# An encoder on one core: the memory's tokens turned by VectorE from row tile 4 on, one row tile at a time

## The chip, the cores and the metric

The kernel runs on one core of a Trainium2 chip. A core has a matrix engine (TensorE, PE in the profile), an elementwise engine (VectorE, DVE), an engine for activations (ScalarE, ACT), a general one (GpSimd, POOL) and one that here only issues transfers (SyncE, SP). Each works through its own instructions in order; they meet through semaphores. The metric is the device time of the whole program in microseconds, lower is better.

## The reference

The program is a two-layer encoder for 256 rows of 2048 numbers. Each layer projects the normed rows, runs three groups of heads (a gated convolution, a differential attention, an attention into 256 memory rows), and adds the projected result.

```python
def rmsnorm(x, g):
    y = x * lax.rsqrt(jnp.mean(x * x, axis=-1, keepdims=True) + EPS)
    return y * g

for l in range(DEPTH):                          # DEPTH = 2
    proj = rmsnorm(x, norm_g[l]) @ w_in[l]      # 256 x 2048 by 2048 x 7168
    y_a = short_gated_conv(a_x, a_b, a_c, conv_w[l], conv_b[l]) * silu(a_g)
    y_d = rmsnorm(diff_attention(q, k, v, lam, slopes), ...) * (1.0 - lam_init) * silu(d_g)
    mkv = rmsnorm(mem, mem_norm_g[l]) @ w_mem_kv[l]     # 256 x 2048 by 2048 x 1024
    mk, mv = rmsnorm(mkv[..., :512], mem_k_norm_g[l]), mkv[..., 512:]
    y_m = memory_attention(rmsnorm(m_q, mem_q_norm_g[l]), mk, mv) * silu(m_g)
    x = x + concat(y_a, y_d, y_m) @ w_out[l]    # 2048 x 2048
```

The change concerns `mkv`, which the kernel computes for both layers before anything else, since the memory is the same for both.

## The kernel before

All products run in a split form: an operand is cut into a high part and a low part (what the high part leaves over), and three products high x high, low x high and high x low are added up. ScalarE makes the high parts, VectorE the low ones.

The memory stage is a loop over `g` = 0 to 31: 16 row tiles of 128 rows of the contraction for layer 0, then 16 for layer 1 (`NG` = 32, `k = g % 16`). For each `g` TensorE does 12 products of 512 columns: two halves of the 1024 columns (keys, values), two tiles of 128 memory rows, three product kinds. Both operands of a row tile must be ready:

- the tokens, transposed, as `memT` (high and low part), made once in layer 0 and kept for layer 1. `token_parts` calls `split_T`, which casts the high part on ScalarE (L261) and subtracts on VectorE (L262).
- the weights. `weights(g + 4)` starts the load of a row tile (512 KB) into one of four `raw` buffers; `w_parts` scales by the norm's gain and makes the high part on ScalarE (L738, tile `hi`) and the low part on VectorE (L739, tile `lo`), each into one of four buffers.

The operands of row tile `g + 2` are made while TensorE works on `g` (`operands`: first the tokens, then the weights). Up to `g` = 2 the loop is written out apart, with the operands of the next tile only.

The tokens come in two ways. Row tiles 0 to 7 (`k < DEALT`, with `DEALT` = 8) are loaded in their natural layout into `xs`, and TensorE transposes them into PSUM (`turned`, L744, two instructions for a row tile). Row tiles 8 to 15 are loaded as strips of 32 rows into a tile `xt` (`strips_of`, four transfers of 128 KB for four row tiles), and one VectorE transpose of 128x1024, which turns blocks of 32x32, yields four row tiles (`strips_turned`, L634, tile `xf`). These row tiles take every fourth row of a block of 512, and their weights and gains (`gm_dealt`) are loaded in the same arrangement. The turn is a task: it is started at `g` = 2 and `g` = 4 and runs some steps later. The rows of `xs` are also needed for the sum of squares, which ScalarE makes in four pairs (`mem_squares`, L681) at `g` = 4, 8, 11 and 13.

At the end of a layer's row tiles the order of the products differs: for `k` = 14 and 15 the first half (keys) of both comes first and the second halves of both behind, and for the first two row tiles of layer 1 likewise, so that ScalarE can empty the first layer's accumulators (`empty_keys`, L782, `empty_values`, L788) meanwhile.

From `g` = 12 on the same loop loads the strips of `x`, turns them in the same way (`x_turned`) and makes `xT` for the first layer's projections; `x_next` does it again at the end of layer 0.

Nearly all of this is pinned: each engine gets its instructions in the order in which the program writes them. SP issues the loads in program order too, and a load into a buffer that is still read holds up those behind it.

Of the kernel before, what the change touches and what calls it, by code (L numbers as in the profile page):

```python
# [37 lines left out]
NA = P // B  # L38
PAIR_EVERY = 9
QT = NB // P  # L40
DEALT = 8


C_X, C_B, C_C, C_G = 0, 768, 1536, 2304
# [5 lines left out]
def encoder(ctx: ExitStack, tc: tile.TileContext, x, mem, norm_g, w_in, conv_w, conv_b,  # L50
# [21 lines left out]
    def nm(s):  # L72
        uid[0] += 1
        return f"{s}_{uid[0]}"
# [54 lines left out]
    def g_norm(l, k):  # L129
        return gx[:, l * KT + k:l * KT + k + 1]  # L130
# [83 lines left out]
    def later(g, n):  # L214
        due[id(g)] = chunk[0] + n
        return g
# [40 lines left out]
    def split_T(dst, k, src, gain, pin=False):  # L257

        hi, lo = dst[:, 0, k, :], dst[:, 1, k, :]
        if gain is None:  # L260
            both = (nc.scalar.copy(hi, src),  # L261
                    nc.vector.tensor_tensor(lo, src, hi.bitcast(F32), ALU.subtract))  # L262
        else:
            both = (nc.scalar.activation(hi, src, AF.Copy, scale=gain),
                    nc.vector.scalar_tensor_tensor(lo, src, gain, hi.bitcast(F32), ALU.mult, ALU.subtract))
        if pin:
            for i in both:
                tc.keep_in_program_order(i)
        made.add((id(dst), k))
# [352 lines left out]
    def strips_of(src, at_once=1):  # L622

        st = tmp.tile([P, SEQ // B, B * QT], F32, tag="e", name=nm("xt"))
        for b in range(NA):
            pin(nc.sync.dma_start(
                st[b * B:(b + 1) * B], src[:, b * B * QT:(b + 1) * B * QT].rearrange("(n p) r -> p n r", p=B)))
            if (b + 1) % at_once == 0 and b + 1 < NA:
                yield
        return st  # L630

    def strips_turned(st):
        whole = tmp.tile([P, QT, SEQ], F32, tag="sh", name=nm("xf"))
        pin(nc.vector.transpose(whole.rearrange("p j (n i) -> p j n i", i=B),  # L634
                                st.rearrange("p n (c j) -> p j n c", j=QT)))
        return whole

    def x_turned(dst, l, q, src, at_once):


        st = yield from strips_of(src, at_once)
        yield 2
        whole = strips_turned(st)
        yield
        for j in range(QT):
            split_T(dst, q * QT + j, whole[:, j], g_norm(l, q * QT + j), pin=True)
            if j % 2:
                yield

    def x_next(dst, l, q):  # L650

# [92 lines left out]
            pin(nc.tensor.transpose(pt[:, t * P:(t + 1) * P], xs[:, t, k * P:(k + 1) * P], ident))  # L744
        return pt

    dealt = {}

    def mem_turned(q, at_once):
        st = yield from strips_of(mem[:, q * NB:(q + 1) * NB], at_once)  # L750
        yield 2
        dealt[q] = strips_turned(st)

    def token_parts(g):
        if g < KT:
# [2 lines left out]
    def operands(g):  # L758
        token_parts(g)
        w_parts(g)  # L760
# [32 lines left out]
    def x_natural(c, t):  # L793
        pin(nc.sync.dma_start(xs[:, t, c * NB:(c + 1) * NB], x[t * P:(t + 1) * P, c * NB:(c + 1) * NB]))

    TOKENS = {0: 4, 1: 6, 8: 8, 9: 10, 10: 12, 11: 14}
    MEM_STRIPS = {2: 2, 4: 3}
    X_STRIPS = {12: 0, 16: 1, 20: 2, 24: 3}
    X_NATURAL = {14: (0, 0), 17: (0, 1), 20: (1, 0), 22: (1, 1), 24: (2, 0), 26: (2, 1), 28: (3, 0), 29: (3, 1)}
    X_SQUARES = {19: 0, 25: 1, 29: 2}  # L800
# [1 line left out]
    def beside(g):  # L802


        if g + 4 < NG:
            if g in TOKENS:
                tokens(TOKENS[g], 2)
            weights(g + 4)
        if g in MEM_STRIPS:
            tasks.append(later(mem_turned(MEM_STRIPS[g], 2 if g == 2 else 1), 1))  # L810
        if g >= 2:
            for dst, src in islice(constants, 1):
                pin(nc.sync.dma_start(dst, src))
        if g in X_STRIPS:
            q = X_STRIPS[g]
            tasks.append(later(x_turned(xT, 0, q, x[:, q * NB:(q + 1) * NB], 1), 1))
        if g in (4, 8, 11, 13):
            mem_squares((4, 8, 11, 13).index(g))
        if g == 6:
            distance(1)  # L820
        if g == 13:
            tasks.append(later(mem_stats(), 1))
        if g == 21:
            tasks.append(later(rest_of_constants(), 1))
        if g in X_NATURAL:
            x_natural(*X_NATURAL[g])
        if g in X_SQUARES:
            for t in range(NT):
                x_square(X_SQUARES[g], t)
# [22 lines left out]
    weights(2, NB, NB)  # L852
    tokens(3, 1)
    weights(3)
    warm(6)
    distance(0)
    pv = ps_t.tile([P, NB], F32, tag="t", name="pva")
# [13 lines left out]
    for g in range(3):  # L871
        if g > 0:
            products(g, 0, FIRST + REST)
        w_parts(g + 1, 0, NB)
        products(g, 1, FIRST)
        token_parts(g + 1)
        w_parts(g + 1, NB, NB)
        beside(g)
        products(g, 1, REST)
        run_side()  # L880
    for g in range(3, NG):
        l, k = divmod(g, KT)
        ends = k >= KT - 2
        begins = l > 0 and k < 2
        products(g, 0, FIRST)
        if begins and k == 1:
            empty_values(0)
        for n in (4, 5) if g == 3 else (g + 2,):
            if n < NG:
                operands(n)  # L890
        products(g, 0, REST)
        beside(g)
        if k == KT - 1:
            empty_keys(l)
        if not (ends or begins):
            products(g, 1, FIRST + REST)
        elif k in (1, KT - 1):
            for n in (g - 1, g):
                products(n, 1, FIRST + REST)
        run_side()  # L900
# [199 lines left out]
```

## Time and profile before

| | us |
|---|---|
| median of 3 runs | 920.24 (919.87 to 920.91) |
| profiled execution | 920.2 |
| its span, first to last instruction | 918.3 |
| TensorE busy | 912.9 (99%) |
| VectorE busy | 675.0 (74%) |
| ScalarE busy | 501.3 (55%) |
| granted TensorE clock | 1.00 throughout |

In the profile's rows a name like `memT<-xf` is the written tile and those read; `L262` is a line of the kernel before. The memory stage takes about the first 95 us of the span, of which layer 0's sixteen row tiles take the first 51. The busy shares are means over the whole program; in a single stage another engine can be the one that is waited for.

### The profile page before, as it was taken

The numbers are of one execution on the slowest core, as the hardware profiler recorded it, in microseconds if no ns is written. First come the engines' busy times: TensorE is split into PE (matmuls) and PEld (weight loads), VectorE is DVE, ScalarE is ACT, GpSimd is POOL, SyncE is SP. The second block draws the span as 40 slices with busy tenths as digits, with TensorE's granted clock in tenths as the row PEclk, the third lists the DMA queues.
The fourth block names the chain that finished last, engine by engine and source line by source line (L and its number), as shares of the span: only waits on it lengthen the run. The fifth ranks groups of instructions, "written<-read, shape, count | busy, mean of one in ns | idle before, by whom it ended". The sixth has DMA issues, their size and how long they took to land.

```text
span 918.3 us, 12315 instructions
## 1 busy us (share of the span) xinstructions
PE 912.9 (99%) x4176; PEld 758.8 (83%) x4176; DVE 675.0 (74%) x1197; ACT 501.3 (55%) x770; POOL 7.0 (1%) x18
## 2 busy tenths in 40 slices
PE   9999999999999999999999999999999999999998
PEld 6888888888888888888888888888888888888886
DVE  5889978867898777458676757878898677458652
ACT  6766745675545654446455544568555554446431
POOL 0001000000000000000000000000000000000000
PEclk9999999999999999999999999999999999999999
DMA  8999878876769997989677767886888897978662
GB/s 283 290 292 299 273 247 233 252 212 184 186 216 256 239 263 227 240 267 260 221 259 246 235 199 219 234 233 185 236 230 222 242 249 215 281 231 252 211 221 74
DMA packets 254242, 216.11 MB, mean 235 GB/s; under 512 B 131982, under 2 KB 181476, under 8 KB 254180
## 3 DMA queue, kind: packets, MB, share of 16 engines
q1 hardware_dynamic: 252020, 211.78, 80.2%
q0 software_dynamic: 672, 2.10, 0.6%
q10 hardware_dynamic: 1488, 1.46, 0.5%
q8 instruction: 32, 0.52, 0.2%
q14 instruction: 30, 0.25, 0.1%
HBM read 194.32 MB, written 20.97 MB: 234 GB/s over the span
## 4 chain that ended last, share of the span: by engine, by line
PE 99%; DMA 0%; ACT 0%; ACTq 0%; DVE 0%; DVEq 0%; issue 0%
PE acc L311 28%; PE acc L312 28%; PE acc L310 28%; PE acc L773 10%; PE po L443 2%; PE s L551 1%; PE s L550 1%; PE s L603 1%; DMA raw<-in_w_mem_kv_dram 0%; PE pt L744 0%; ACT hi L738 0%; ACTq L842 0%; DVE xs L1061 0%; DVEq L1095 0%; PE pvb L150 0%
## 5 line engine op out<-in xcount | busy, mean ns | idle before, releaser
L290 DVE TENSOR_TENSOR lo<-raw,hi 128x1024 fp32r<-128x1024 f32 x288 | 351.6, 1222 | 181.2 <-ACT hi L289 176.4
L289 ACT CAST hi<-raw 128x1024 fp32r<-128x1024 f32 x288 | 302.4, 1052 | 327.1 <-PE acc L312 263.7
L311 PE MATMUL acc<-lo,xT 128*128 128x512 f32 x896 | 349.0, 390 | 0.0
L312 PE MATMUL acc<-hi,xT 128*128 128x512 f32 x896 | 348.7, 389 | 0.0
L310 PE MATMUL acc<-hi,xT 128*128 128x512 f32 x896 | 348.4, 391 | 0.0
L312 PEld LDWEIGHTS acc<-hi,xT 128*128 128x128 f32 x896 | 168.2, 188 | 34.9
L310 PEld LDWEIGHTS acc<-hi,xT 128*128 128x128 f32 x896 | 168.2, 188 | 33.9
L311 PEld LDWEIGHTS acc<-lo,xT 128*128 128x128 f32 x896 | 168.3, 188 | 33.5
L310 PE MATMUL acc<-hi,yT 128*128 128x512 f32 x256 | 99.6, 389 | 0.0
L311 PE MATMUL acc<-lo,yT 128*128 128x512 f32 x256 | 99.6, 389 | 0.0
L312 PE MATMUL acc<-hi,yT 128*128 128x512 f32 x256 | 99.6, 389 | 0.0
L773 PE MATMUL acc<-hi,memT 128*128 128x512 f32 (+1 forms) x260 | 70.5, 389 | 0.7 <-ACT hi L738 0.7
L773 PEld LDWEIGHTS acc<-hi,memT 128*128 128x128 f32 x260 | 47.9, 188 | 10.8 <-ACT hi L738 1.2
L311 PEld LDWEIGHTS acc<-lo,yT 128*128 128x128 f32 x256 | 48.0, 188 | 10.1
L310 PEld LDWEIGHTS acc<-hi,yT 128*128 128x128 f32 x256 | 48.0, 188 | 10.0
L312 PEld LDWEIGHTS acc<-hi,yT 128*128 128x128 f32 x256 | 48.0, 188 | 9.8
L773 PE MATMUL acc<-lo,memT 128*128 128x512 f32 (+1 forms) x130 | 39.7, 387 | 0.0
L773 PEld LDWEIGHTS acc<-lo,memT 128*128 128x128 f32 x130 | 24.3, 188 | 5.0
L739 DVE SCALAR_TENSOR_TENSOR lo<-raw,cva,hi 128x1024 fp32r<-128x1024 f32 (+2 forms) x21 | 21.4, 1027 | 5.9 <-ACT hi L738 4.8
L561 ACT ACTIVATE e<-e,mx 128x256 f32<-128x256 f32 x48 | 23.8, 498 | 1.4 <-DVE mx L557 1.3
L739 DVE SCALAR_TENSOR_TENSOR lo<-raw,gm_dealt,hi 128x1024 fp32r<-128x1024 f32 x16 | 20.5, 1279 | 4.1 <-ACT hi L738 3.4
L738 ACT ACTIVATE hi<-raw,cva 128x1024 fp32r<-128x1024 f32 (+2 forms) x21 | 19.6, 947 | 5.1 <-DMA raw<-in_w_mem_kv_dram 5.1
(155 smaller groups left out, 634.5 us busy)
## 6 DMA issues: line engine op xcount, KB each, us to landing
raw<-in_w_in_dram SPq DMA_DIRECT2D x192, 512.0 KB, 4.3
raw<-in_w_out_dram SPq DMA_DIRECT2D x64, 512.0 KB, 4.5
raw<-in_w_in_dram SPq DMA_DIRECT2D x64, 256.0 KB, 4.4
raw<-in_w_mem_kv_dram SPq DMA_DIRECT2D x29, 512.0 KB, 5.9
d<-sh SPq DMA_DIRECT2D x80, 128.0 KB, 3.9
sh<-d SPq DMA_DIRECT2D x64, 128.0 KB, 3.8
d<-yn SPq DMA_DIRECT2D x40, 64.0 KB, 3.9
yn<-d SPq DMA_DIRECT2D x40, 64.0 KB, 3.3
```

Source lines behind the costliest of these rows:

```text
L289: nc.scalar.copy(hi, raw)
L290: nc.vector.tensor_tensor(lo_, raw, hi.bitcast(F32), ALU.subtract)
L310: nc.tensor.matmul(acc[t], sh, hi, start=first, stop=False)
L311: nc.tensor.matmul(acc[t], sh, lo, start=False, stop=False)
L312: nc.tensor.matmul(acc[t], sl, hi, start=False, stop=last)
L443: nc.tensor.matmul(po[:, t, :], eT[:, i, t, k, :], v[:, k, h * P:(h + 1) * P], start=k == 0, stop=k == NT - 1)
L550: nc.tensor.matmul(s[c][:, i, :], qi, k_first(yT, c, h), start=True, stop=False)
L551: nc.tensor.matmul(s[c][:, i, :], qi, k_second(yT, k2, c, h), start=False, stop=True)
L561: nc.scalar.activation(e[:, c, i], e[:, c, i], AF.Exp, bias=mx[:, c, i:i + 1], accum_out=sm[:, c, i:i + 1])
L738: pin(nc.scalar.activation(hi, raw, AF.Copy, scale=gain))
L739: pin(nc.vector.scalar_tensor_tensor(lo, raw, gain, hi.bitcast(F32), ALU.mult, ALU.subtract))
L773: pin(nc.tensor.matmul(accs[l, half][t][:, at:at + n], memT[:, token_part, k, t * P:(t + 1) * P], p, start=k == 0 and at == 0 and token_pa ...
```

## The change

`DEALT` becomes 4: row tiles 4 to 7 also come in strips, and TensorE transposes only row tiles 0 to 3. Their strips are loaded ahead of the loop, right behind the weights of row tile 3, and one of the two gain loads with them. VectorE no longer turns four row tiles of the memory at once: `mem_turn(k)` turns a single one (128x256), row tile 4 at `g` = 2 and each later one behind the operands of the row tile before it. The strips of `x` are turned in halves of two row tiles (128x512). The natural tokens of row tiles 4 to 7, now needed for the squares alone, are loaded later, and the squares move to `g` = 4, 10, 12 and 14.

```diff
-DEALT = 8
+DEALT = 4
...
-    def strips_turned(st):
-        whole = tmp.tile([P, QT, SEQ], F32, tag="sh", name=nm("xf"))
-        pin(nc.vector.transpose(whole.rearrange("p j (n i) -> p j n i", i=B),
-                                st.rearrange("p n (c j) -> p j n c", j=QT)))
-        return whole
+    def turn_strips(whole, st, at, n):
+        pin(nc.vector.transpose(whole.rearrange("p j (n i) -> p j n i", i=B)[:, at:at + n],
+                                st.rearrange("p n (c j) -> p j n c", j=QT)[:, at:at + n]))
...
-        whole = strips_turned(st)
-        yield
-        for j in range(QT):
-            split_T(dst, q * QT + j, whole[:, j], g_norm(l, q * QT + j), pin=True)
-            if j % 2:
-                yield
+        whole = whole_tile()
+        for j in range(0, QT, 2):
+            turn_strips(whole, st, j, 2)
+            yield
+            for i in (j, j + 1):
+                split_T(dst, q * QT + i, whole[:, i], g_norm(l, q * QT + i), pin=True)
...
+    def mem_strips(q, at_once):
+        strips_in[q] = yield from strips_of(mem[:, q * NB:(q + 1) * NB], at_once)
+
+    def mem_turn(k):
+        q, j = divmod(k, QT)
+        if j == 0:
+            dealt[q] = whole_tile()
+        turn_strips(dealt[q], strips_in[q], j, 1)
...
-    TOKENS = {0: 4, 1: 6, 8: 8, 9: 10, 10: 12, 11: 14}
-    MEM_STRIPS = {2: 2, 4: 3}
+    TOKENS = {4: 4, 7: 6, 8: 8, 9: 10, 10: 12, 11: 14}
+    MEM_STRIPS = {2: 2, 5: 3}
...
-        if g in (4, 8, 11, 13):
-            mem_squares((4, 8, 11, 13).index(g))
+        if g in (4, 10, 12, 14):
+            mem_squares((4, 10, 12, 14).index(g))
...
     weights(3)
+    for _ in mem_strips(1, NA):
+        pass
+    for dst, src in islice(constants, 1):
+        pin(nc.sync.dma_start(dst, src))
...
         products(g, 1, FIRST)
+        if g + 2 == DEALT:
+            mem_turn(DEALT)
         token_parts(g + 1)
...
                 operands(n)
+            if n + 1 < KT:
+                mem_turn(n + 1)
```

How this moves the instructions is seen best in the built order. First VectorE, before, around the operands of row tiles 6 to 9 (`memT` from `pt` or `xf` is the tokens' low part, `lo` the weights' low part, the STREAM_TRANSPOSE the turn of the strips `xt`):

```order
L739 SCALAR_TENSOR_TENSOR lo_295<-raw_242,cva,hi_294 128x1024
L262 TENSOR_TENSOR memT_105<-pt_319,memT_105 128x256
L739 SCALAR_TENSOR_TENSOR lo_325<-raw_276,cva,hi_324 128x1024
L634 STREAM_TRANSPOSE xf_341<-xt_249 128x1024
L262 TENSOR_TENSOR memT_105<-xf_341,memT_105 128x256
L739 SCALAR_TENSOR_TENSOR lo_349<-raw_302,gm_dealt,hi_348 128x1024
L262 TENSOR_TENSOR memT_105<-xf_341,memT_105 128x256
L739 SCALAR_TENSOR_TENSOR lo_372<-raw_332,gm_dealt,hi_371 128x1024
```

In the changed kernel VectorE has this around the operands of row tiles 3 to 6:

```order
L740 SCALAR_TENSOR_TENSOR lo_235<-raw_126,cva,hi_234 128x512
L636 STREAM_TRANSPOSE xf_240<-xt_128 128x256
L262 TENSOR_TENSOR memT_105<-pt_242,memT_105 128x256
L740 SCALAR_TENSOR_TENSOR lo_235<-raw_126,cva,hi_234 128x512
L262 TENSOR_TENSOR memT_105<-xf_240,memT_105 128x256
L740 SCALAR_TENSOR_TENSOR lo_264<-raw_196,gm_dealt,hi_263 128x1024
L636 STREAM_TRANSPOSE xf_240<-xt_128 128x256
L262 TENSOR_TENSOR memT_105<-xf_240,memT_105 128x256
L740 SCALAR_TENSOR_TENSOR lo_271<-raw_221,gm_dealt,hi_270 128x1024
L636 STREAM_TRANSPOSE xf_240<-xt_128 128x256
```

Before, one turn stands between the operands of row tiles 7 and 8 and none between 8 and 9; now a turn of a quarter of the size stands between those of every two row tiles from 3 on, each behind the low part of the weights and ahead of the low part of the tokens that it yields. On ScalarE, which makes the high parts, the same place (row tiles 3 to 5) reads before

```order
L738 ACTIVATE hi_229<-raw_126,cva 128x512
L261 CAST memT_105<-pt_254 128x256
L738 ACTIVATE hi_259<-raw_191,cva 128x1024
L261 CAST memT_105<-pt_263 128x256
L738 ACTIVATE hi_268<-raw_217,cva 128x1024
L261 CAST memT_105<-pt_289 128x256
```

and now

```order
L261 CAST memT_105<-pt_242 128x256
L739 ACTIVATE hi_234<-raw_126,cva 128x512
L261 CAST memT_105<-xf_240 128x256
L739 ACTIVATE hi_263<-raw_196,gm_dealt 128x1024
L261 CAST memT_105<-xf_240 128x256
L739 ACTIVATE hi_270<-raw_221,gm_dealt 128x1024
```

The order is the same: each cast of tokens stands between the high part of the weights before it and that of its own row tile. What is new is that the casts read `xf`, which VectorE turned, where they read `pt`, which TensorE transposed. The third place is SP's queue around the weights of row tiles 3 to 6 (`raw_126` are those of row tile 3), before

```order
L731 DMA raw_126<-in_w_mem_kv_dram 128x1024
L721 DMA xs<-in_mem_dram 128x2x256
L731 DMA raw_191<-in_w_mem_kv_dram 128x1024
L721 DMA xs<-in_mem_dram 128x2x256
L731 DMA raw_217<-in_w_mem_kv_dram 128x1024
L731 DMA raw_242<-in_w_mem_kv_dram 128x1024
L813 DMA gm_dealt<-in_mem_norm_g_dram 128x2x4
L626 DMA xt_249<-in_mem_dram 32x8x128 x2
```

and now

```order
L732 DMA raw_126<-in_w_mem_kv_dram 128x1024
L626 DMA xt_128<-in_mem_dram 32x8x128 x4
L863 DMA gm_dealt<-in_mem_norm_g_dram 128x3x4
L732 DMA raw_196<-in_w_mem_kv_dram 128x1024
L732 DMA raw_221<-in_w_mem_kv_dram 128x1024
L818 DMA gm_dealt<-in_mem_norm_g_dram 128x3x4
L732 DMA raw_249<-in_w_mem_kv_dram 128x1024
```

The loads of natural tokens around the weights of row tile 4 are gone from here, and four strips and a gain load stand ahead of those weights.

More of the change, by code (lines that the diff above doesn't have):

```diff
@@ L630, in strips_of, with whole_tile @@
         return st
-    def strips_turned(st):
-        whole = tmp.tile([P, QT, SEQ], F32, tag="sh", name=nm("xf"))
-        pin(nc.vector.transpose(whole.rearrange("p j (n i) -> p j n i", i=B),
-                                st.rearrange("p n (c j) -> p j n c", j=QT)))
-        return whole
+    def whole_tile():
+        return tmp.tile([P, QT, SEQ], F32, tag="sh", name=nm("xf"))
+    def turn_strips(whole, st, at, n):
+        pin(nc.vector.transpose(whole.rearrange("p j (n i) -> p j n i", i=B)[:, at:at + n],
+                                st.rearrange("p n (c j) -> p j n c", j=QT)[:, at:at + n]))
     def x_turned(dst, l, q, src, at_once):
@@ L745, in turned @@
         return pt
[L747 to L752, printed above, removed]
+    dealt, strips_in = {}, {}
+    def mem_strips(q, at_once):
[5 more added lines that the diff above has]
+        turn_strips(dealt[q], strips_in[q], j, 1)
     def token_parts(g):
@@ L809, in beside @@
         if g in MEM_STRIPS:
-            tasks.append(later(mem_turned(MEM_STRIPS[g], 2 if g == 2 else 1), 1))
-        if g >= 2:
+            tasks.append(later(mem_strips(MEM_STRIPS[g], 2), 1))
+        if g >= 1:
             for dst, src in islice(constants, 1):
@@ L816, in beside @@
             tasks.append(later(x_turned(xT, 0, q, x[:, q * NB:(q + 1) * NB], 1), 1))
-        if g in (4, 8, 11, 13):
-            mem_squares((4, 8, 11, 13).index(g))
+        if g in (4, 10, 12, 14):
+            mem_squares((4, 10, 12, 14).index(g))
         if g == 6:
             distance(1)
-        if g == 13:
+        if g == 14:
             tasks.append(later(mem_stats(), 1))
```

## The prediction

> **What bounds the kernel now.** I read the page first: the busy times and the chain that ended last.
>
> ```profile
> span 918.3 us, 12315 instructions
> PE 912.9 (99%) x4176; PEld 758.8 (83%) x4176; DVE 675.0 (74%) x1197; ACT 501.3 (55%) x770; POOL 7.0 (1%) x18
> PE 99%; DMA 0%; ACT 0%; ACTq 0%; DVE 0%; DVEq 0%; issue 0%
> ```
>
> TensorE is busy for 912.9 of 918.3 us and holds 99% of the chain. So there are only two ways to move the time: take work from TensorE, or make it wait. The second view is the chain in order of time, in the memory stage (start, us, what).
>
> ```profile
> 14.05 1.40 PE acc L773 x6
> 15.45 0.44 PE pt L744 x4
> 15.89 2.77 PE acc L773 x12
> 18.66 0.22 PE pt L744 x2
> 18.88 2.77 PE acc L773 x12
> 21.66 0.22 PE pt L744 x2
> 21.88 45.84 PE acc L773 x202
> ```
>
> From 21.88 on 202 products take 45.84 us, 0.227 each, and the 12 of a row tile 2.72 us. This is the pace that the other engines must hold. The third view is the timeline of DVE and ACT where the turn of tiles 12 to 15 stands today (start, us, and in brackets the idle time before and what ended it).
>
> ```profile
> 33.67 1.28 DVE L739 SCALAR_TENSOR_TENSOR lo<-raw,gm_dealt,hi 128x1024 fp32r<-128x1024 f32 x1 [0.63 <-ACT hi L738]
> 34.87 1.98 DVE L634 STREAM_TRANSPOSE xf<-xt 128x1024 f32<-128x1024 f32 x1
> 36.88 0.41 ACT L261 CAST memT<-xf 128x256 fp32r<-128x256 f32 x1 [3.25 <-DVE xf L634]
> 37.20 1.15 ACT L738 ACTIVATE hi<-raw,gm_dealt 128x1024 fp32r<-128x1024 f32 x1
> 38.38 1.29 DVE L739 SCALAR_TENSOR_TENSOR lo<-raw,gm_dealt,hi 128x1024 fp32r<-128x1024 f32 x1 [0.63 <-ACT hi L738]
> 38.54 1.15 ACT L738 ACTIVATE hi<-raw,gm_dealt 128x1024 fp32r<-128x1024 f32 x1
> 39.58 0.42 DVE L262 TENSOR_TENSOR memT<-xf,memT 128x256 fp32r<-128x256 f32 x1
> 39.60 0.62 ACT L681 ACTIVATE msq<-xs 128x512 f32<-128x512 f32 x1
> 40.82 0.39 ACT L261 CAST memT<-xf 128x256 fp32r<-128x256 f32 x1
> ```
>
> Here is a closed path. The weight's low part on DVE (33.67) must finish before the turn behind it (34.87); ACT's cast of the tokens waits for the turn (3.25 us idle); the weight's high part follows the cast on ACT; the next low part on DVE waits for that high part. Today the path closes once in four tiles: the low parts of tile 11 and tile 12 start 4.71 us apart, and the three other tiles of the quarter make it up.
>
> **The change part by part.**
>
> *Removed: eight transposes on TensorE* (tiles 4 to 7, two each). From 15.45 to 21.88 lie 6.43 us with 24 products; 24 x 0.227 = 5.45, so the eight cost 0.98 us with the breaks in the pipeline. They lie on the chain: -0.98.
>
> *Added: a turn of 128x256 behind every tile's low part*, twelve in place of two of 128x1024. This is the part that counts. No turn of 128x256 is in the trace; the nearest rows are these (us in all, mean ns).
>
> ```profile
> L634 DVE STREAM_TRANSPOSE xf<-xt 128x1024 f32<-128x1024 f32 x10 | 20.1, 2009 | 0.0
> L405 DVE STREAM_TRANSPOSE sh<-sh 128x1024 f32<-128x1024 f32 x10 | 12.4, 1238 | 0.0
> L534 DVE STREAM_TRANSPOSE yn<-yn 128x512 f32<-128x512 f32 x10 | 7.0, 700 | 0.0
> ```
>
> The plain turns cost 1238 for 1024 elements and 700 for 512, so 162 ns of each are fixed. A quarter of the 2009 with the fixed part kept is (2009 - 162) / 4 + 162 = 624 ns. The bounds: 502 if nothing were fixed, 431 if the small turn ran at the plain pace (162 + 1076 / 4). Nothing below that is likely, since all these rows move the same kind of data. I take 624, because the plain rows show the fixed part directly. [...]
>
> Now the path closes in every tile, since the order puts tile n+1's turn behind tile n's low part, and the cast of tile n+1 behind tile n's high part. Its period, from the third view: 1.20 from low part to turn (33.67 to 34.87); the turn; 1.53 from the turn's end (34.87 + 1.98 = 36.85) over cast and high part to the next low part (38.38). That is 2.73 + 0.62 = 3.35 us, against TensorE's 2.72. Each tile loses 0.63 us, and nothing later in the loop gives it back. The cover that hid the turn so far was the three tiles without one.
>
> How much lead there is at the start comes from the rows around tile 3.
>
> ```profile
> 12.13 1.49 DVE L739 SCALAR_TENSOR_TENSOR lo<-raw,cva,hi 128x512 fp32r<-128x512 f32 x2 [0.20 <-ACT hi L738]
> 14.36 0.73 ACT L738 ACTIVATE hi<-raw,cva 128x512 fp32r<-128x512 f32 x1
> 14.83 0.62 PE L773 MATMUL acc<-hi,memT 128*128 128x512 f32 x2
> ```
>
> The turn of tile 4 stands behind the low parts that end at 13.62. ACT is free for tile 4's cast at 15.09, makes the high part from 15.41 to 16.56, and DVE's low part of tile 4 starts at 16.59. TensorE begins tile 3 at 14.83, so without waits tile 4 at 17.55, tile 14 at 44.77, and, as the second halves of tiles 14 and 15 are put off behind both first halves, tile 15 only 6 products (1.36) later, at 46.13. It needs a tile's low part after 4 products, 0.91 later: for tile 15 at 47.04. The low part of tile 15 starts at 16.59 + 11 x 3.354 = 53.48 and ends 1.28 later, at 54.76. So TensorE comes out **7.7 us late**: 11 x 0.63 lost, 1.36 for the short tile 14, less 0.6 of lead at tile 4. After tile 15 no turn follows and the path opens.
>
> *What follows at once.* Behind tile 15 ACT has to empty the accumulators of the first layer before TensorE may fill them for the second.
>
> ```profile
> 48.48 1.07 ACT L782 COPY kraw<-acc 128x512 f32<-128x512 f32 x2
> 49.44 0.65 ACT L360 ACTIVATE sq<-kraw 128x512 f32<-128x512 f32 x1
> 51.54 1.27 ACT L788 ACTIVATE mv<-acc,stm 128x512 f32<-128x512 f32 x2
> ```
>
> With no lead left, ACT goes from the high part of tile 15 (ends near 53.4) through high parts 16 to 18, the moved pair of squares, both copies and two squares (3 x 1.06 + 1.22 + 1.07 + 2 x 0.6) (a high part 1.06 from start to start, 38.54 to 39.60) to about 60.1 and gives the first value accumulator back near 60.7, the second near 61.4. TensorE, 14 products after 54.76, wants them 12 products later, at 60.7. The second is late: **+0.5**, between 0 and 1.3 (both copies).
>
> *Moved: tokens and weights in SP's queue.* Four strip loads and one gain load now stand ahead of the weights of tile 4.
>
> ```profile
> 6.39 0.43 SPq L721 DMA_DIRECT2D xs<-in_mem_dram  x1
> 9.92 3.32 SPq L731 DMA_DIRECT2D raw<-in_w_mem_kv_dram  x2
> xt<-in_mem_dram SPq DMA_DIRECT2D x8, 128.0 KB, 5.9
> DMA to landing us min/median/max: 4.9/5.8/7.3
> ```
>
> The strips take the place of the load at 6.39; at about 0.45 each the last goes out near 8.2 and lands 5.9 later, at 14.1. The turn is over at 14.7, ahead of ACT at 15.09: no cost. At the slowest landing, 7.3, the path starts 1.0 later, and the weights of tile 4, out near 9.2, can then be as late: 0 to +1.1, I take 0. The weights of tile 5 went out at 9.92 already and keep that place. Later strips wait for a turn to free their buffer, and the weights queued behind them on SP are used 10 us later: 0.
>
> *Squares and the rest.* A pair of squares takes 1.22 on ACT (39.60 to 40.82), and ACT idles 1.9 in each turn of the closed path (low part and turn): 0; without that cover the three moved pairs would cost up to 3.7. The halves of x add a fixed 0.16 to each of eight quarters, 1.3 if all lay bare. There the waits between 465 and 535 us (who waits for whom, us, times, longest) show ACT ahead of TensorE, waiting for it to free buffers:
>
> ```profile
> ACT hi L289 <- PE acc L312: 27.8, 18, 1.7
> ```
>
> So that is 0 as well.
>
> **Sum.** 918.3 - 0.98 + 7.7 + 0.5 = 925.5 us of span. The profiled execution took 920.2, 1.9 around its span, and the median of the runs is 920.24; so 927.4 us, 0.8% slower.
>
> **The rivals.**
>
> *The turn stays hidden* (not slower). If DVE did the turn while it waits for ACT's high part (the 0.63 idle before each low part), nothing would close: ACT needs 0.32 + 1.06 per tile (cast and high part, start to start), DVE 1.20 + 0.42 + 0.62 (low part, the tokens' low part as at 39.58, turn), both below 2.72. For it: those sums. Against it: the turn stands behind the low part in the order, and an engine works in order. Time 920.2 - 1.0 = 919.2. It decides if the path's period is under 2.72, which a turn of any length forbids.
>
> *Only the strips are late.* The loads miss ACT's 15.09 by 1.0 and the path is otherwise hidden: 920.2. For it, the 7.3 landing; against it, the median.
>
> *The clock falls.* The page shows full clock throughout, but no regular gaps. Before the array is warm 6 products take 2.72:
>
> ```profile
> 0.79 2.72 PE L125 MATMUL warm<-const-bfloat16-1.0 128*128 128x512 bf16 x6 [0.79 <-PEq L1086]
> 5.54 1.14 PE L773 MATMUL acc<-hi,memT 128*128 128x256 f32 x6 [0.74 <-ACT hi L738]
> 7.23 0.62 PE L773 MATMUL acc<-hi,memT 128*128 128x512 f32 x2
> ```
>
> At that 0.45 a tile takes 5.44 and eleven tiles 29.9 more: 949. Against it: after the 0.74 gap at 5.54 the products run at full pace (two in 0.62 at 7.23). [...]
>
> **How the numbers follow.** What a measurement of this kernel can tell from no change is 0.2%, 1.8 us. Closed path, 927.4: 0.82. Turn hidden, 919.2: 0.08, and late strips alone, 920.2: 0.04, both within 0.2%. Clock, 949: 0.03. For something faster that I don't see: 0.03. So slower 0.85, same 0.12, faster 0.03. The closed path's own bounds: a turn of 431 takes 11 x 0.19 = 2.1 off, the emptying 0.5, so 924.8; late loads add 1.1 and the emptying 0.8, so 929.3. To leave out no more than 2 in 10 I widen this to 922.5 to 930.
>
> **What would show it.** Right: TensorE idle some 0.6 us before most of tiles 6 to 15, ended by DVE's low parts; about 7 to 8 us of that in the waits; ACT's cast waiting for the turn near 1.9 us a tile; turns of 128x256 near 624 ns; products within a tile still 0.227 apart. Wrong: TensorE without gaps up to 50 us (turn hidden), gaps that end with a load (strips), products at 0.45 (clock), or a time under 922.

## The result, and the profile after

| | before | after |
|---|---|---|
| median (lowest to highest), us | 920.58 (919.87 to 921.72), 6 runs | 929.66 (928.92 to 932.78), 6 runs |
| after / before | | 1.0108, 95% interval 1.0096 to 1.0119 |
| profiled execution, and its span, us | 920.2, 918.3 | 932.78, 931.0 |
| granted TensorE clock | 1.00 | 1.00 |

The change makes the kernel 9.1 us slower by the medians, 9.9 by the ratio. Single runs far off (1318 to 5156 us), one each of e7, e8, e12 and e13 and one of before, are in medians but in no ratio. The profiled execution of after is the slowest of its six; the spans of the other five lie between 927.1 and 930.0. The page of after first: the busy times, and the chain that ended last.

```profile
span 931.0 us, 12325 instructions
PE 920.0 (99%) x4168; PEld 755.9 (81%) x4168; DVE 679.4 (73%) x1215; ACT 501.6 (54%) x770; POOL 7.0 (1%) x18
PE 91%; DMA 3%; DVE 3%; ACT 2%; issue 1%; SPq 0%; DVEq 0%; ACTq 0%
```

TensorE held 99% of the chain before; now DMA, DVE and ACT hold 8%. TensorE's busy time rose by 7.1 us with eight instructions fewer, so a part of its waiting is counted as busy time, and its 99% says little here. The timeline of VectorE shows the closed path (start, us, and in brackets the idle time before and what ended it):

```profile
15.13 0.63 DVE L636 STREAM_TRANSPOSE xf<-xt 128x256 f32<-128x256 f32 x1 [0.96 <-DMA xt<-in_mem_dram]
...
17.67 1.29 DVE L740 SCALAR_TENSOR_TENSOR lo<-raw,gm_dealt,hi 128x1024 fp32r<-128x1024 f32 x1 [0.61 <-ACT hi L739]
18.87 0.63 DVE L636 STREAM_TRANSPOSE xf<-xt 128x256 f32<-128x256 f32 x1
21.03 1.28 DVE L740 SCALAR_TENSOR_TENSOR lo<-raw,gm_dealt,hi 128x1024 fp32r<-128x1024 f32 x1 [0.63 <-ACT hi L739]
22.23 0.63 DVE L636 STREAM_TRANSPOSE xf<-xt 128x256 f32<-128x256 f32 x1
24.39 1.28 DVE L740 SCALAR_TENSOR_TENSOR lo<-raw,gm_dealt,hi 128x1024 fp32r<-128x1024 f32 x1 [0.63 <-ACT hi L739]
```

Low parts start 3.36 us apart (17.67, 21.03, 24.39), each turn 1.20 behind its low part, each low part 0.63 after DVE fell idle. ScalarE closes the path; between two closings it is idle for 1.90, until the turn:

```profile
15.80 0.41 ACT L261 CAST memT<-xf 128x256 fp32r<-128x256 f32 x1 [0.81 <-DVE xf L636]
16.49 1.15 ACT L739 ACTIVATE hi<-raw,gm_dealt 128x1024 fp32r<-128x1024 f32 x1 [0.28 <-DMA raw<-in_w_mem_kv_dram]
19.54 0.41 ACT L261 CAST memT<-xf 128x256 fp32r<-128x256 f32 x1 [1.90 <-DVE xf L636]
19.85 1.15 ACT L739 ACTIVATE hi<-raw,gm_dealt 128x1024 fp32r<-128x1024 f32 x1
22.89 0.41 ACT L261 CAST memT<-xf 128x256 fp32r<-128x256 f32 x1 [1.90 <-DVE xf L636]
```

The view of groups has the sizes of the turns (us in all, mean ns), and the view of waits the sums over the first 105 us (who waits for whom: us, times, longest):

```profile
L636 DVE STREAM_TRANSPOSE xf<-xt 128x256 f32<-128x256 f32 x12 | 7.5, 627 | 1.0 <-DMA xt<-in_mem_dram 1.0
L636 DVE STREAM_TRANSPOSE xf<-xt 128x512 f32<-128x512 f32 x16 | 17.5, 1096 | 0.0
```

```profile
ACT memT L261 <- DVE xf L636: 17.7, 12, 1.9
ACT hi L739 <- DMA raw<-in_w_mem_kv_dram: 9.5, 10, 1.9
PEld acc L778 <- DVE lo L740: 8.0, 14, 0.9
PEld acc L778 <- ACT hi L739: 7.1, 13, 1.7
ACT sq L671 <- DMA xs<-in_x_dram: 6.8, 3, 2.3
ACT hi L289 <- DMA raw<-in_w_in_dram: 2.3, 1, 2.3
```

How late TensorE comes out is read at two places of its timeline. First the low products of row tile 15, before (L773) and after (L778):

```profile
48.06 0.62 PE L773 MATMUL acc<-lo,memT 128*128 128x512 f32 x2
```

```profile
54.62 1.20 PE L778 MATMUL acc<-hi,memT 128*128 128x512 f32 x4 [1.30 <-ACT hi L739]
55.94 0.74 PE L778 MATMUL acc<-lo,memT 128*128 128x512 f32 x2
```

They are 7.88 us late. Then, before and after, the same products behind the emptied accumulators (55.31 and 63.52) and the first product of the projections of `x` (L310):

```profile
55.31 1.07 PE L773 MATMUL acc<-hi,memT 128*128 128x512 f32 x4
...
95.18 0.39 PE L310 MATMUL acc<-hi,xT 128*128 128x512 f32 x1
```

```profile
63.52 0.85 PE L778 MATMUL acc<-hi,memT 128*128 128x512 f32 x3
...
87.67 1.20 PE L778 MATMUL acc<-hi,memT 128*128 128x512 f32 x4 [0.42 <-ACT hi L739]
89.34 0.73 PE L778 MATMUL acc<-lo,memT 128*128 128x512 f32 x2 [0.48 <-DVE lo L740]
107.50 0.50 PE L310 MATMUL acc<-hi,xT 128*128 128x512 f32 x1 [1.51 <-ACT kraw L787]
```

They are 8.21 and 12.32 late. So in this execution 0.3 went at the accumulators, and 4.1 between 63 and 107 us. ScalarE's timeline shows where:

```profile
84.95 0.63 ACT L671 ACTIVATE sq<-xs 128x512 f32<-128x512 f32 x1 [2.28 <-DMA xs<-in_x_dram]
...
86.48 2.20 ACT L739 ACTIVATE hi<-raw,gm_dealt 128x1024 fp32r<-128x1024 f32 x2
...
105.92 1.05 ACT L289 CAST hi<-raw 128x1024 fp32r<-128x1024 f32 x1 [0.62 <-DMA raw<-in_w_in_dram]
106.87 1.07 ACT L787 COPY kraw<-acc 128x512 f32<-128x512 f32 x2
```

The gap at 87.67 ends with a high part (86.48) whose row shows no wait for weights: it stood on ScalarE behind a square of `x` (84.95) that had waited 2.28 for its rows. Such waits of squares come to 6.8 us in the change. Before they were

```profile
ACT sq L670 <- DMA xs<-in_x_dram: 2.2, 2, 1.9
```

At 107.50 TensorE waits for ScalarE to empty the keys of layer 1 (106.87), which stands behind a high part of the first projection's weights that waited for its load. So it is loads of three kinds that come late: the memory's weights, the rows of `x` and the projection's weights. The rest of the span, some 823 us, is alike (12.7 of difference in span). The loss therefore has two parts: one of about 8 us up to row tile 15, a little in every row tile; and one behind it.

### The profile page after: what moved, and what is told of

Read it like the earlier page. It is cut to its first block, busy times and chain, and to the rows that moved or that the text cites. A ratio compares the mean times of both kernels' runs of the same rounds, so it can differ in the third digit from the quotient of the medians.

```text
span 931.0 us, 12325 instructions
## 1 busy us (share of the span) xinstructions
PE 920.0 (99%) x4168; PEld 755.9 (81%) x4168; DVE 679.4 (73%) x1215; ACT 501.6 (54%) x770; POOL 7.0 (1%) x18
## 4 chain that ended last, share of the span: by engine, by line
PE 91%; DMA 3%; DVE 3%; ACT 2%; issue 1%; SPq 0%; DVEq 0%; ACTq 0%
PE acc L310 28%; PE acc L311 28%; PE acc L312 28%; PE acc L778 2%; PE po L443 2%; DVE lo L740 2%; ACT hi L739 1%; DMA xs<-in_x_dram 1%; DMA raw<-in_w_in_dram 1%; DMA raw<-in_w_mem_kv_dram 1%; DVE xf L636 1%; PE s L551 1%; PE s L550 1%; PE s L603 1%; DMA xs<-in_mem_dram 0%
## 5 line engine op out<-in xcount | busy, mean ns | idle before, releaser
L310 PE MATMUL acc<-hi,xT 128*128 128x512 f32 x896 | 348.4, 391 | 1.5 <-ACT kraw L787 1.5
L310 PEld LDWEIGHTS acc<-hi,xT 128*128 128x128 f32 x896 | 168.2, 188 | 35.7 <-ACT kraw L787 1.9
L310 PE MATMUL acc<-hi,yT 128*128 128x512 f32 x256 | 99.6, 389 | 0.0
L778 PE MATMUL acc<-hi,memT 128*128 128x512 f32 (+1 forms) x260 | 72.0, 396 | 2.7 <-ACT hi L739 1.9
L778 PEld LDWEIGHTS acc<-hi,memT 128*128 128x128 f32 x260 | 47.0, 188 | 17.8 <-ACT hi L739 7.1
L310 PEld LDWEIGHTS acc<-hi,yT 128*128 128x128 f32 x256 | 48.1, 188 | 10.0
L312 PEld LDWEIGHTS acc<-hi,yT 128*128 128x128 f32 x256 | 48.1, 188 | 10.0
L311 PEld LDWEIGHTS acc<-lo,yT 128*128 128x128 f32 x256 | 48.1, 188 | 9.8
L778 PE MATMUL acc<-lo,memT 128*128 128x512 f32 (+1 forms) x130 | 41.4, 399 | 1.9 <-DVE lo L740 0.5
L740 DVE SCALAR_TENSOR_TENSOR lo<-raw,gm_dealt,hi 128x1024 fp32r<-128x1024 f32 x24 | 30.7, 1280 | 10.8 <-ACT hi L739 10.0
L778 PEld LDWEIGHTS acc<-lo,memT 128*128 128x128 f32 x130 | 23.2, 188 | 12.0 <-DVE lo L740 8.0
L739 ACT ACTIVATE hi<-raw,gm_dealt 128x1024 fp32r<-128x1024 f32 x24 | 27.5, 1148 | 8.4 <-DMA raw<-in_w_mem_kv_dram 8.4
L636 DVE STREAM_TRANSPOSE xf<-xt 128x512 f32<-128x512 f32 (+1 forms) x28 | 25.1, 895 | 1.0 <-DMA xt<-in_mem_dram 1.0
```

The source lines that it names most:

```text
L310: nc.tensor.matmul(acc[t], sh, hi, start=first, stop=False)
L311: nc.tensor.matmul(acc[t], sh, lo, start=False, stop=False)
L312: nc.tensor.matmul(acc[t], sl, hi, start=False, stop=last)
L739: pin(nc.scalar.activation(hi, raw, AF.Copy, scale=gain))
L740: pin(nc.vector.scalar_tensor_tensor(lo, raw, gain, hi.bitcast(F32), ALU.mult, ALU.subtract))
L778: pin(nc.tensor.matmul(accs[l, half][t][:, at:at + n], memT[:, token_part, k, t * P:(t + 1) * P], p, start=k == 0 and at == 0 and token_pa ...
```

## Experiments on the closed path

Theory: the order low part, turn, cast, high part, low part closes through two engines that work in order, and its period is the loss. Rival: VectorE simply has too much to do for a row tile, wherever the turn stands. In each case the time is a median, and the ratio is that to the kernel before on the same chip, with its 95% interval.

**The turn ahead of the low part** (e1).

```diff
-                operands(n)
-            if n + 1 < KT:
-                mem_turn(n + 1)
+                token_parts(n)
+                if n + 1 < KT:
+                    mem_turn(n + 1)
+                w_parts(n)
```

> The turn of row tile n+1 stands ahead of the weights' low part of row tile n on VectorE, all else as in the change. Closed path (low part, turn, cast, high part): the turn now falls into the 0.63 us in which VectorE waits for ScalarE, the period drops below 2.72 us, and of the change's cost only the late strips at row tile 3 (0.8) stay against the 0.98 saved: 920 us, and with the lead back no loss in the strips of x either. If the late loads, the second load of the tokens, or the halves of x cost the time: 925 to 930, with gaps on TensorE that do not come every 3.36 us.

Measured 925.41 us, 1.0046 (1.0028 to 1.0064): 4.2 us better than the change by the medians, 5.7 by the ratios, and 5 short of the forecast. The gaps of every 3.36 us are gone from TensorE's timeline, and the casts' waits for turns fall from 17.7 us to 2.4. In their place are loads that land late; the waits from 10 to 105 us, and the rows of TensorE that a late operand ended:

```profile
ACT hi L739 <- DMA raw<-in_w_mem_kv_dram: 15.5, 13, 2.7
ACT sq L671 <- DMA xs<-in_x_dram: 6.5, 3, 2.3
```

```profile
29.59 1.19 PE L778 MATMUL acc<-hi,memT 128*128 128x512 f32 x4 [0.90 <-ACT hi L739]
...
78.68 0.73 PE L778 MATMUL acc<-lo,memT 128*128 128x512 f32 x2 [0.43 <-DVE lo L740]
81.23 1.20 PE L778 MATMUL acc<-hi,memT 128*128 128x512 f32 x4 [0.44 <-ACT hi L739]
82.91 0.73 PE L778 MATMUL acc<-lo,memT 128*128 128x512 f32 x2 [0.48 <-DVE lo L740]
100.41 0.50 PE L310 MATMUL acc<-hi,xT 128*128 128x512 f32 x1 [1.14 <-ACT kraw L787]
```

The gap at 29.59 comes from weights, for which ScalarE waited 2.74; those at 81 and 83 stand behind a square that waited 2.00 for rows of `x`. The sum of the waits for weights alone tells little: in e8 below, where TensorE does not wait, it is 13.1 in the same stretch, with 3.0 for rows of `x`.

**Eight row tiles turned singly, behind (e3) and ahead of (e8) the low part.** The kernel before, where only row tiles 8 to 15 come in strips, with the change's `mem_turn`. The diff is e8's; in e3 the turn stands behind `w_parts`.

```diff
...
-                operands(n)
+                token_parts(n)
+                if DEALT <= n + 1 < KT:
+                    mem_turn(n + 1)
+                w_parts(n)
```

> The kernel before, with row tiles 8 to 15 turned one at a time behind the low part of the row tile before; x whole, squares and loads as before. Closed path: low part of tile 7 at 23.37 us, eight periods of 3.36, so tile 15's low part ends at 51.5 instead of the 48.06 at which TensorE needs it: 3.5 us late, 0.5 for the accumulators, 924.2; if the lost lead also lets the loads of x through, 0.5 to 4 more. If the singles cost nothing: 920.2.

> The kernel before with row tiles 8 to 15 turned one at a time as in the earlier run of that kind (924.03 us), but each turn issued ahead of the low part of the weights of its turn, not behind it; no extra load. Theory of the closed path from low part to turn to cast to high part: 920.2 to 921 us, the gaps of 0.4 to 0.6 us on TensorE every 3.36 us gone. Rival, that VectorE's own work for each row tile is the limit, wherever the turn stands: 924 us.

Measured 924.03 us, 1.0036 (1.0023 to 1.0049), and 920.22 us, 0.9994 (0.9984 to 1.0004). Both met their numbers. Same work on the same engines in both, and TensorE from 30 to 60 us reads (columns: PE, PEld, DVE, ACT, POOL busy, clock, DMA share, GB/s), behind and ahead:

```profile
30.00:60.00 30.00, 28.28 (x118) 21.15 (x117) 21.98 (x39) 20.76 (x35) 0.00 (x0) 1.00 0.79 242
```

```profile
30.00:60.00 30.00, 30.00 (x134) 24.86 (x133) 23.43 (x40) 22.25 (x36) 0.00 (x0) 1.00 1.05 297
```

118 against 134 products. VectorE is idle for 8 of the 30 us in the slow one (21.98 busy, against 23.43), so the rival falls: with turns of the same length in both, it is the place of the turn in the order that costs the time.

**Quarter turns at the first single's place** (e4). The change with one 128x1024 turn for four row tiles, issued where the first single turn of the four stands.

```diff
         if j == 0:
             dealt[q] = whole_tile()
-        turn_strips(dealt[q], strips_in[q], j, 1)
+            turn_strips(dealt[q], strips_in[q], 0, QT)
```

> The change with the memory's strips turned a quarter at a time (128x1024) where the first single turn of the quarter stood. Closed path: it closes once in four tiles and the three others make it up; the first turn takes 2.0 instead of 0.63 and holds up tile 3 by 2.2 in place of 0.8: 921.4. If the number of strips or loads costs the time and not the place of the turns: 928 to 930.

Measured 927.65 us, 1.0080 (1.0063 to 1.0098), 6 us over the forecast. Here a turn takes 2.0 us, and the first stands in TensorE's way directly:

```profile
16.56 0.73 PE L778 MATMUL acc<-hi,memT 128*128 128x512 f32 x2 [1.30 <-DVE memT L262]
42.04 1.19 PE L778 MATMUL acc<-hi,memT 128*128 128x512 f32 x4 [0.56 <-ACT hi L739]
...
101.71 0.50 PE L310 MATMUL acc<-hi,xT 128*128 128x512 f32 x1 [0.69 <-ACT kraw L787]
```

A miss: the forecast had left out both the first turn's wait for strips and the late loads behind it. With e1 it suggests that a second loss, some 5 to 6 us (what the two lie above their forecasts), comes with row tiles 4 to 7 and not with the place or number of the turns.

## Experiments on the late weights

What follows asks what makes the loads late. The change does five more things, and each could hold up the weights: a second load of tokens, weights' rows taken four apart, half turns of `x`, strips ahead of the loop, small constants two row tiles earlier. Each was taken out of the kernel with the turn ahead (925.41), or put into one without the loss (e8, 920.22), or both.

**The second load of tokens** (row tiles 4 to 7 in their natural layout, 0.5 MB, for the squares alone). Taken out of the kernel with the turn ahead (e5) and of the change (e6), and put into the kernel before (e7).

```diff
...
-    TOKENS = {4: 4, 7: 6, 8: 8, 9: 10, 10: 12, 11: 14}
+    TOKENS = {8: 8, 9: 10, 10: 12, 11: 14}
...
```

> The kernel with the single turns ahead of the weights' low parts (925.41 us, 1.0046 of before), less the second load of the tokens of row tiles 4 to 7 in their natural layout, 0.5 MB. Left out of the computation: the squares of columns 512 to 1023 are taken from columns 0 to 511 again, as many squares of the same size. Theory that the second load delays the weights of the x strips' stage: 920 to 921.5 us, and ScalarE's waits on raw weights ahead of 100 us fall back from 16.5 us towards the 6.1 us of before. Rival, that the place of the turns or the lost lead delays them: 925.4 us as with the load.

> The change itself less the same second load of 0.5 MB, with the squares of columns 512 to 1023 taken from columns 0 to 511 again. Theory of two separate losses (closed path 7.9 us and 0.5 us at the accumulators, the second load the rest): 927.0 to 928.0 us, the first matmul on an x block at about 103.5 us. Rival, that the load costs nothing: 929.7 us. Rival, that the load makes the closed path's loss as well: near 921 us.

```diff
+        if g in (4, 7):
+            tokens(4 if g == 4 else 6, 2)
...
```

> The kernel before, with the tokens of row tiles 4 to 7 loaded a second time in their natural layout, 0.5 MB behind the weights of row tiles 8 and 11, and the squares as late as in the change; nothing is left out and VectorE turns what it turned before. Theory that the second load delays the weights: 922 to 925 us, the time lost between 60 and 105 us. Rival, that the load is hidden as long as the strips come early: 920.5 us.

Measured 925.07 us, 1.0034 (1.0020 to 1.0049), against 1.0046 with the load; 928.87 us, 1.0089 (1.0073 to 1.0104), against 1.0108; and 921.23 us, 1.0005 (0.9996 to 1.0014). My theory of that point said the load was the whole second loss; it falls. By the ratios each pair differs by 0.5 to 1.8 us, and none by more than its intervals allow.

**Half turns of x**, whole again in the change (e2), whole in the kernel with the turn ahead (e16), halves put into e8 (e18), and whole without the second load (e17).

```diff
-        for j in range(0, QT, 2):
-            turn_strips(whole, st, j, 2)
-            yield
-            for i in (j, j + 1):
-                split_T(dst, q * QT + i, whole[:, i], g_norm(l, q * QT + i), pin=True)
+        turn_strips(whole, st, 0, QT)
+        yield
+        for i in range(QT):
+            split_T(dst, q * QT + i, whole[:, i], g_norm(l, q * QT + i), pin=True)
+            if i % 2:
+                yield
```

> The change with the strips of x turned whole again, as before the change. If the loss between 85 and 108 us comes from the lead being gone while the loads of x fill the queue: 929 to 931 as with the change. If it comes from x in halves: 926 to 927.

> The change with its turns ahead of the low parts (925.41 us), with x's strips turned whole as before and not in halves. Theory that the second half-turn holds the strips' buffer some 5 us longer, and that SyncE's queue waits for it with the weights behind: 922 to 923.5 us, SyncE's wait for the turn (2.1 us) gone, and what is lost stays between 28 and 60 us. Rival, that the halves cost nothing: 925.4 us.

> The kernel with eight single turns ahead of the low parts (920.22 us), with x's strips turned in halves as in the change; nothing else is changed. Theory of the held buffer: 921.5 to 923 us, SyncE waiting for a turn between 60 and 80 us and weights landing late behind it. Rival, that the lead of the weights covers the wait: 920.2 us.

> The same with x's strips turned whole and without the second load of the tokens of row tiles 4 to 7 (0.5 MB); the squares of columns 512 to 1023 are taken from columns 0 to 511 again. Theory that halves and second load share the rest of the loss: 920.3 to 921.5 us. Rival, that either alone does it: as the run with x whole alone. Rival, that neither does: 925 us.

Measured 929.32 us, 1.0094 (1.0080 to 1.0108); 924.39 us, 1.0040 (1.0024 to 1.0055); 920.64 us, 1.0005 (0.9996 to 1.0013); 923.6 us, 1.0031 (1.0016 to 1.0046). The mechanism that e16 tested is in the traces: with the halves SyncE's queue waits for a half-turn to free the strips' buffer, and the weights stand behind. From e18, the waits of that queue between 45 and 100 us:

```profile
SPq L626 <- DVE xf L636: 2.3, 1, 2.3
```

But e18 pays nothing that can be measured for it: its weights have a lead that covers the wait, and TensorE's timeline from 10 to 110 us has no idle time. Without a lead it costs some 0.6 us by the ratios (e16 against e1), which the intervals do not tell from nothing.

**Rows of the weights taken four apart**, put into e8 (e9), taken out of the kernel with the turn ahead (e10) and of the change (e11). One line, `if k < DEALT` in `weights`, with 4 and 8 in its place.

> The kernel with eight single turns ahead of the low parts (920.22 us), with the weights of row tiles 4 to 7 and 20 to 23 loaded as the change loads them: a packet of 4 KB from every fourth row, 16 KB apart, and not from rows that follow each other. Their products pair other rows, so the output isn't the reference's; every instruction and every byte count is that of the earlier kernel. Theory that rows taken four apart move slower through a full DMA: 922 to 925 us, the time lost ahead of the first x block. Rival, that only the strips' early landing costs time: 920.2 us.

> The change with its turns ahead of the low parts (925.41 us), with the weights of row tiles 4 to 7 and 20 to 23 loaded from rows that follow each other, as before; their products pair other rows. Theory that rows four apart are slow: 920.5 to 922 us. Rival, that the strips for row tiles 4 to 7 are what delays the weights: 925.4 us.

> The change itself with the weights of row tiles 4 to 7 and 20 to 23 loaded from rows that follow each other, as before; their products pair other rows. Theory that rows four apart are slow: 928 to 929 us, the closed path's 8.4 us left and the loss behind row tile 16 gone. Rival, that the rows cost nothing: 929.7 us.

Measured 920.53 us, 1.0003 (0.9994 to 1.0012); 924.64 us, 1.0046 (1.0030 to 1.0062); 931.34 us, 1.0117 (1.0091 to 1.0142). It is not the rows.

**Small constants two row tiles earlier**, moved back in the kernel with the turn ahead (e13) and in the change (e15), put into e8 (e14).

```diff
-        if g >= 1:
+        if g >= 3:
             for dst, src in islice(constants, 1):
```

> The change with its turns ahead of the low parts (925.41 us), with the small constants behind the first gain (the second layer's gain, the norm gains and the vectors of line 818) issued from row tile 3 on, where the kernel before issues them, and not from row tile 1; the first gain stays early, since row tile 4 needs it. Theory that the early small packets take the weights' lead away: 920.5 to 922 us, and ScalarE's waits on raw weights ahead of 100 us well under 16.5 us. Rival, that the early strips together with the faster TensorE do it: 925 us.

> The kernel with eight single turns ahead of the low parts (920.22 us), with its small constants issued as early as the change issues them: the first gain behind the weights of row tile 3, the others from row tile 1 on. No byte more is loaded. Theory that the early small packets take the weights' lead away: 923 to 925 us. Rival, that they cost nothing by themselves: 920.2 us.

> The change itself with the small constants behind the first gain issued from row tile 3 on. Theory of the early small packets: 928 to 929 us, the closed path's 8.4 us left and the spread between runs (928.9 to 932.8) smaller. Rival, that the closed path hides the constants: 929.7 us.

Measured 925.99 us, 1.0057 (1.0044 to 1.0070); 920.26 us, 1.0001 (0.9992 to 1.0009); 930.34 us, 1.0105 (1.0091 to 1.0120). It is not the constants.

**Early strips alone** (e12), loaded into e8 and read by nothing.

```diff
     weights(3)
+    for _ in mem_strips(1, NA):
+        pass
```

> The kernel with eight single turns ahead of the low parts (920.22 us), with the strips of row tiles 4 to 7 loaded as well, 0.5 MB in four transfers behind the weights of row tile 3, where the change loads them; nothing reads them and nothing else is changed. Theory that the early strips push back the weights: 923 to 925 us, TensorE waiting from row tile 4 on. Rival, that rows four apart are the cause: 920 to 921 us.

Measured 921.61 us, 1.0012 (1.0003 to 1.0022): 1.4 us over e8, the only one of the five pieces whose addition gave an interval off 1, and that barely. Its profiled execution (919.97, the fastest of its twelve) shows no loss: TensorE has no idle time from 10 to 110 us. What the strips do to the transfers shows between 10 and 14 us (the columns as above), in before, in e12, and in the change:

```profile
10.00:14.00 4.00, 4.00 (x21) 3.26 (x20) 2.47 (x4) 1.72 (x3) 0.00 (x0) 1.00 1.05 392
```

```profile
10.00:14.00 4.00, 4.00 (x21) 3.26 (x20) 2.18 (x4) 1.87 (x4) 0.00 (x0) 1.00 1.17 260
```

```profile
10.00:14.00 4.00, 4.00 (x21) 3.24 (x20) 2.20 (x4) 1.73 (x4) 0.00 (x0) 1.00 1.16 221
```

All are at full DMA share (1.05, 1.17 and 1.16), and move 392, 260 and 221 GB/s. In e12 the 4 us at 260 are 1.04 MB; if all four strips (0.52 MB) fall into them, the other 0.52 MB takes 1.33 us at 392, and the strips 2.67: twice the time of as many bytes at before's 392, an estimate from these two rows. In the change, 221 in place of 392 is 0.68 MB less in these 4 us, more than a row tile's weights. From the start to 95 us the kernel before had moved 27.9 MB, the kernel with the turn ahead 26.2 and the change 24.0; but e12, which has the same strips, had moved 28.4, so it made up for them. Less by 95 us is thus not the strips' doing alone. The weights' loads also wait for the low parts that free their buffers (up to 105 us 23.9 us in the change; in before 14.7, and 8.6 for the tokens' low parts), and that a late TensorE adds to this was the author's estimate, which no run shows. The view of transfers up to 95 us, in that order:

```profile
DMA packets 19433, 27.90 MB, mean 294 GB/s; under 512 B 3102, under 2 KB 12660, under 8 KB 19427
```

```profile
DMA packets 19768, 26.24 MB, mean 276 GB/s; under 512 B 3356, under 2 KB 13938, under 8 KB 19762
```

```profile
DMA packets 18526, 23.98 MB, mean 252 GB/s; under 512 B 3215, under 2 KB 13507, under 8 KB 18520
```

```profile
DMA packets 20481, 28.35 MB, mean 298 GB/s; under 512 B 3166, under 2 KB 13748, under 8 KB 20475
```

**What stays open.** The five kernels with eight turns ahead, whatever was added (e8, e9, e12, e14, e18), give 0.9994 to 1.0012; the six with twelve turns ahead, whatever was taken away (e1, e5, e10, e13, e16, e17), 1.0031 to 1.0057. So what is lost comes with row tiles 4 to 7 being turned by VectorE from strips, and no single attached piece carries it. Between e8 and e1 lie 4.8 us by the ratios. If the pieces add up, which no run shows, the early strips are 1.7 of them (e12 over e8), halves and second load together perhaps 1.4 (e1 over e17, with intervals that overlap), and some 1.7 were not located. The cause of the second loss stays open. Three candidates were not tried: strips spread over all partitions; a TensorE that is as slow in row tiles 4 to 7 as the transposes made it; and squares of `x` that do not stand ahead of the weights' high parts on ScalarE.

No kernel beat the one before; e8, the nearest, equals it.

## Why the prediction was right in its mechanism and wrong in its size

Forecast 927.4 us, from 922.5 to 930; the kernel takes 929.66, 1.0108 times the one before. Set on the 920.24 from which the forecast started, that ratio gives 930.2, just past the range.

**The turn of 128x256**: forecast 624 ns, measured 627. The fixed part of 162 ns read off the two plain turns was right. The halves of `x` took 1096, twice that 2192 against 2009 for a whole: 183 ns more a quarter, forecast 160.

**The closed path**: right in mechanism and period. Forecast 3.354, measured 3.36; ScalarE idle 1.90 in every round, forecast 1.9. That the order closes the path is shown by e3 against e8, with turns of the same length: 3.8 us for eight row tiles, gone when the turn moves ahead.

**Its start: here the first term failed.** The prediction said of the strips, and of the weights of tile 4 behind them, "0 to +1.1, I take 0". It let the last strip land at 14.1. The turn of tile 4 could start only at 15.13, after 0.96 of waiting for the strips; ScalarE's cast came at 15.80 and not at 15.09; its high part waited 0.28 more for the weights of tile 4; and the low part began at 17.67 instead of 16.59: 1.08 late. Everything behind carries this: tile 15's low part started at 54.60 against a forecast of 53.48. Against before, TensorE was to be 6.7 late at tile 15 (7.7 less the 0.98 of the transposes) and was 7.88. The median landing of 5.9 us came from strips that went out one or two at a time between weights; four in a row took longer (7.2, after's view of `xt` from 5 to 20 us).

The same products in four relatives of the change that keep the closed path (e2, e6, e11, e15) start at 56.39, 55.13, 55.39 and 55.33, against a forecast of 54.76. In e6, e11 and e15 the turn of tile 4 waits 1.10 to 1.12 for its strips, and they are 0.4 to 0.6 late. In e2 it waits for none: there TensorE came to the transposes of row tile 3 at 15.32, against 13.57 in the change. In the profiled execution of e8, which has no early strips, it came to them at 15.29. So the first 10 us vary between executions by more than this term, and e2 says nothing of it.

**The accumulators**: forecast +0.5, between 0 and 1.3; measured 0.3.

**The rest of the stage: here the second term failed.** "Squares and the rest", which ended with "So that is 0 as well", argued from the waits at 465 to 535 us, where the weights are ahead of TensorE. Between 60 and 107 us they are not: DMA runs at a share of 1.03 and ScalarE waits for loads. (The share alone doesn't tell: before had 0.98 from 60 to 95 us and lost nothing.) The prediction named the second load in no term, gave the weights queued behind later strips 0, because they "are used 10 us later", and counted squares by ScalarE's time for them, not by their wait for rows that land late (6.8 us in the change, 4.0 to 5.7 in the four relatives). From tile 15 to the first product on `x` the kernel before takes 95.18 - 48.06 = 47.1 us. The change took 51.6, e2 49.0, e6 48.1, e11 47.6 and e15 49.5; less 0.3 at the accumulators for each, that is a loss of 0.2 to 4.1, and it is what these runs differ in most. What makes the loads late stays open, as said above.

**The sum, redone** with 0.7 us for the start (the mean of the change, e6, e11 and e15), 0.3 for the accumulators and 1.7 for the rest (the mean of all five): 918.3 - 0.98 + 7.7 + 0.7 + 0.3 + 1.7 = 927.7 of span, 929.6 us. These sizes were put in afterwards, and four of the five kernels differ from the change in other ways too, so that the sum comes near 929.66 proves little. The forecast lay 2.3 under the result because two terms that could only add were both set to 0.

**The rivals.** The turn hidden (919.2) and strips alone (920.2) are out: the gaps are there. The clock stayed at 1.00 through ten rounds that each lost 0.64 us of 3.36 (3.36 less 2.72), and the 12 products of a round come to 0.28 each with its gaps, against the 0.45 of the first six of the program, so the rival of a falling clock is out for gaps of this length. The longest idle time in after's rows is 1.51; what a longer one would do was not shown, nor why the first six are slower, at a granted clock of 1.00 as well.

**What the experiments add to it**: removing the closed path wins back 4.2 to 5.7 us of its 8, since loads that are late anyway then become the bound. A forecast that all of it comes back (e1's 920) failed for that reason.

## What to carry to other kernels

When a task on one engine moves behind another engine's input, draw the order as a loop (who waits for whom, in program order) and add up one round; a loop that closes once per tile costs its excess over the pace in every tile (here 3.36 less 2.72 us), however idle the engines in it are, and moving the task ahead of the waiting instruction opens it (3.8 us from e3 to e8). In a stage where the DMA share is near 1, a load that is added or moved ahead can have a price (1.4 us in e12), though most of those tried here had none that could be measured; a bound of "0 to x" there should not enter the sum as 0. Look also at what an engine waits for ahead of the instruction that matters: squares that waited for rows of `x` (2.28 us ahead of the gap at 87.67) held up high parts that waited for nothing else. Ask for each new lead or lag what the second resource, here the transfers, would then allow.

## What the runs showed of the hardware

- In e12 four transfers into 32 partitions in rows of 512 bytes (0.52 MB) took 2.67 us at a DMA share of 1.17, by the estimate above, which makes 196 GB/s, against 392 before: about twice the time of as many bytes. The 221 of the change are not to be compared, since other loads fall into the same 4 us. What this comes from, the few partitions, the short rows or something else, no run here shows.
- In a kernel whose weights have a lead, a second load of 0.5 MB gave 1.0005 (0.9996 to 1.0014), the half turns 1.0005 (0.9996 to 1.0013): nothing that can be measured. Without the lead the time also varies more from run to run: 921.0 to 926.6 us in the twelve runs of e5, against 919.7 to 922.5 in eleven of e8's twelve.
